# Adding DMAs for the low halves in units 2 to 10 of a decoder layer's feed-forward input, and a fourth pair by seven products in each

## The chip, the cores and the metric

The kernel runs on one core of one Trainium2 chip. The metric is the device time of one execution in microseconds (us); lower is better.

## The reference

One layer of a decoder trunk works on a sequence of 256 rows of 2048 float32 values. It has a token mixer (three kinds of attention with one combined input projection) and then a gated feed-forward part. Only the feed-forward input matters here:

```
gate, up = split(h @ w_ffn_in)        # h: 256 x 2048, w_ffn_in: 2048 x 11264
x = x + gate2 * ((silu(gate) * up) @ w_ffn_out)
```

`h` is the normalised input of this part; gate and up have 5632 columns each.

## The kernel before

**Products in two halves.** TensorE multiplies in a rounded float32 format. To keep the accuracy, each operand is split: a high half (the operand rounded, made by a cast on ScalarE) and a low half (operand minus high half, a subtraction on VectorE). One product of a 128 x 128 piece of `h` and a 128 x 512 piece of a weight is then three matmuls, in `mm3`, lines 172 to 174: high x high, high x low of the weight (L173), low x high.

**Units.** The 5632 columns of gate and of up are done in 11 units of 512 columns. A unit takes 512 columns of gate (`c0`) and the same of up (`c1`), over all 2048 rows of the weight. These rows are 16 pieces of 128, in 8 pairs. Units 0 and 1 run through `block`. Units 2 to 10 (`FAST`) run through `fast_products`, which takes the pairs in the order of a list; each entry of the list is a pair's number and a flag.

- A pair with flag 0 is done *plainly*: two column blocks (gate's, then up's) x two row tiles of `h` x two pieces = 8 products, 24 matmuls. Its two weight blocks of 128 x 1024 values are loaded, cast and subtracted one after the other. The text calls them the pair's first and second block.
- A pair with flag 1 is done *by seven products*, in Strassen's manner: 21 matmuls. For it VectorE first makes sums and differences of the weight blocks (four subtractions of 128 x 512), and then there are three splits of 128 x 1024 and one of 128 x 512. The first of the seven products is collected over all such pairs of the unit in the accumulator `p1`; when the last such pair is done, `p1` is copied on ScalarE (L1430) and four additions on VectorE combine the rest (L1431 to L1434); the halves of the result are added in `merge` (L1390).

Units 2, 3, 5, 6 and 8 (`FOUR`) have four pairs by seven products and four plain (`PAIRS_4`), the units 4, 7, 9 and 10 three and five (`PAIRS`). In both lists a unit's first two pairs are plain.

**Where blocks live.** `load_pair` brings a pair in. `raw_at` (L1334) issues a 512 KB load on SyncE's queue into a buffer for raw weights, of which there are six in turn up to unit 8, five in unit 9 and four in unit 10. `split` takes the next pair of tiles for the two halves, in the text also a room (`whi` and `wlo`, four of each, and further pairs of old tiles: `X1`/`X2` and `A2`/`A3` in all units, `A4`/`A8` up to unit 9, `T4`/`T5` up to unit 6); so there are eight rooms up to unit 6, seven in units 7 to 9 and six in unit 10. It issues the cast on ScalarE (L1354) and the subtraction on VectorE (L1340, through `sub`). A room is free again when TensorE has read both halves for the last time; a raw buffer, when the subtraction has read it.

**Order.** Each engine works through its instructions in one order that the framework's scheduler writes at build time, from priorities; an instruction that waits holds those behind it on its engine. SyncE's loads are such a queue too. GpSimd's queue has nothing in units 2 to 10 but, as unit 2 begins, the last of six DMAs of 512 KB that put tiles away in DRAM (L1239 for `x2`, L1253 for the second gate's sums).

Of the kernel before, what the change touches and what calls it, by code (L numbers as in the profile page):

```python
# [10 lines left out]
F32 = mybir.dt.float32  # L11
# [3 lines left out]
ALU = mybir.AluOpType  # L15
# [7 lines left out]
DFF = 5632  # L23
NB = 512
# [23 lines left out]
OUT_UNITS = (4, 5, 6, 3)  # L48
OUT_A = tuple((p, 0) for p in range(8)) + tuple(x for i in range(6) for x in ((8 + i, 1), (14 + i, 0))) + ((20, 0), (21, 0))
OUT_B = ((0, 0), (1, 0)) + tuple(x for a, b in zip((8, 9, 10, 11, 12, 13, 6, 7), (2, 3, 4, 5, 14, 15, 16, 17)) for x in ((a, 1), (b, 0)))  # L50
PAIRS = ((0, 0), (1, 0), (5, 1), (2, 0), (6, 1), (7, 1), (3, 0), (4, 0))
PAIRS_4 = ((0, 0), (1, 0), (4, 1), (5, 1), (2, 0), (6, 1), (7, 1), (3, 0))
FOUR = (2, 3, 5, 6, 8)
RANK = 16
ROW_N1, ROW_N2, ROW_SBQ, ROW_SBK, ROW_DILQ, ROW_DILK, ROW_GB, ROW_GG = 16, 32, 48, 49, 50, 51, 52, 56

# [23 lines left out]
def trunk(ctx: ExitStack, tc: tile.TileContext, I, out):  # L80
    nc = tc.nc
# [11 lines left out]
    def nm(base):  # L93
        uid[0] += 1
        return f"{base}_{uid[0]}"

    def S(tag, shape, dtype=F32):
        return slot.tile(shape, dtype, tag=tag, name=nm(tag))
# [4 lines left out]
    def scr(shape, dtype=F32):  # L103
        return sp.tile(shape, dtype, tag="scr", name=nm("scr"))

    def acc_bank(shape=None):
        return psa.tile(shape or [P, NB], F32, tag="acc", name=nm("acc"))
# [4 lines left out]
    @contextmanager  # L112
    def prio(offset=AHEAD):

        with tc.high_priority(offset=offset):
            start = tc.cur_priority
            yield
            n = tc.cur_priority - start
        tc.cur_priority += n

    state = {"rate": 0.0}
# [12 lines left out]
    def flush():  # L134
        while bg or after:
            tick(1)


    def load_weights(src, k0, k1, c0, w=NB, spare=(), ahead=True, late=None):

        parts = []
        step = (2 * NB) // w
        with prio() if ahead else nullcontext():
            for ka in range(k0, k1, step):
                n = min(step, k1 - ka)
                raw = wp.tile([P, step, w], F32, tag="raw", name=nm("raw"))
                state["load"] = nc.sync.dma_start(  # L150
                    raw[:, :n, :],
                    src[ka * P : (ka + n) * P, c0 : c0 + w].rearrange("(k p) c -> p k c", p=P),
                )
                i = len(spare) - (k1 - ka)
                if i >= 0:
                    hi = S(spare[i], [P, step, w], F32R)
                    lo = S(spare[i + 1], [P, step, w], F32R)
                else:
                    hi = wp.tile([P, step, w], F32R, tag="whi", name=nm("whi"), bufs=4)
                    lo = wp.tile([P, step, w], F32R, tag="wlo", name=nm("wlo"), bufs=4)  # L160
                if i >= 0 and late is not None:
                    state["casts_after"] = late
                with tc.issue_after(state["casts_after"]) if "casts_after" in state else nullcontext():
                    state["cast"] = nc.scalar.copy(hi[:, :n, :], raw[:, :n, :])  # L164
                state["split"] = nc.vector.tensor_tensor(lo[:, :n, :], raw[:, :n, :], hi[:, :n, :].bitcast(F32), op=ALU.subtract)  # L165
                parts += [(hi[:, i, :], lo[:, i, :]) for i in range(n)]
        if late is not None:
            state.pop("casts_after", None)
        return parts
# [928 lines left out]
    for j in range(2):  # L1098
        hi = S(gtag[0][j], [P, 4, T], F32R)
        lo = S(gtag[1][j], [P, 4, T], F32R)  # L1100
        for t in range(NT):
# [5 lines left out]
            for par in range(2):  # L1107
                gcol = vec[:, ROW_GG + par : ROW_GG + par + 1]
                src = ps[:, par:4:2, :]
# [195 lines left out]
    w_ff = I["w_ffn_in"]  # L1305
# [21 lines left out]
    def load_pair(src, p, c0, c1, fast, tags):  # L1327


        def raw_at(c):  # L1330
            more_raws = state.get("more_raws", ())
            i = state["raws"] = (state.get("raws", -1) + 1) % (4 + len(more_raws))
            raw = S(more_raws[i], [P, 2, NB]) if i < len(more_raws) else wp.tile([P, 2, NB], F32, tag="raw", name=nm("raw"))
            nc.sync.dma_start(raw, src[2 * p * P : (2 * p + 2) * P, c : c + NB].rearrange("(k p) c -> p k c", p=P))  # L1334
            return raw

        def sub(dst, x, y):
            chain = state.get("chain")
            with tc.issue_after(chain.ins) if chain is not None else nullcontext():
                done = nc.vector.tensor_tensor(dst, x, y, op=ALU.subtract)  # L1340
            if "chain" in state:
                state["chain"] = done
            return done

        def split(src):
            n = src.shape[1]
            more_rooms = state.get("more_rooms", ())
            i = state["tiles"] = (state.get("tiles", -1) + 1) % (4 + len(more_rooms))
            if i < len(more_rooms):
                hi, lo = (S(tag, [P, 2, NB], F32R) for tag in more_rooms[i])  # L1350
            else:
                hi = wp.tile([P, 2, NB], F32R, tag="whi", name=nm("whi"), bufs=4)
                lo = wp.tile([P, 2, NB], F32R, tag="wlo", name=nm("wlo"), bufs=4)
            nc.scalar.copy(hi[:, :n, :], src)  # L1354
            state["split"] = sub(lo[:, :n, :], src, hi[:, :n, :].bitcast(F32))
            return [(hi[:, i, :], lo[:, i, :]) for i in range(n)]

        with prio():
            if not fast:
                return [split(raw_at(c0)), split(raw_at(c1))]  # L1360
            r0, r1 = raw_at(c0), raw_at(c1)
            b11, b21 = split(r0)
            ta, tb = (S(tag, [P, 2, NB]) for tag in tags)
            sub(ta[:, 0], r1[:, 0], r0[:, 0])
            sub(ta[:, 1], r1[:, 1], r1[:, 0])
            (b22,) = split(r1[:, 1:2])
            sub(tb[:, 0], r1[:, 1], ta[:, 0])
            sub(tb[:, 1], r0[:, 1], tb[:, 0])
            t1, t3 = split(ta)
            t2, t4 = split(tb)  # L1370
            return b11, b21, b22, t1, t3, t2, t4
# [71 lines left out]
    def rooms_until(i, rooms):  # L1443
        return tuple(tags for tags, end in rooms if i < end)

    def fast_unit(i):
        own, other = (acc_bank, misc_bank) if i % 2 else (misc_bank, acc_bank)
        return fast_products(w_ff, i * NB, DFF + i * NB, PAIRS_4 if i in FOUR else PAIRS, h2_at, h2s, own, other, ("OD", "KD"))

    ring["tags"] = ("A12", "KD", "KC", "T0", "A7", "A11")  # L1450
    act = []
    for i in range(NFF):
        if i == FAST[0]:
            flush()
        state["more_rooms"], state["more_raws"] = rooms_until(i, MORE_ROOMS), rooms_until(i, MORE_RAWS)
        if i in FAST:
            pg, pu = fast_unit(i)
        else:
            state["rate"] = RATES_FFN[2 * i]
            pg = [acc_bank() for _ in range(NT)]  # L1460
        if i in FAST:
            pass
        elif i == 0:
            w = load_weights(w_ff, 0, KC, 0, spare=("A9", "A10", "A0", "A1", "T1", "T2", "T4", "T5"), late=state["late_casts"])
            state["loads_after"] = state["load"].ins
            for t in range(NT):
                block(pg, h2_at, None, 0, KC, 0, w=w, tiles=(t,), steps=None if t else {N2_AT[1]: lambda: norm2_turn(1, xs)}, pace=0.5)
        else:
            block(pg, h2_at, w_ff, 0, KC, i * NB)
        if i == 0:  # L1470
            h2s = sums_of_h2()
        sgs = []
        with prio():
            for t in range(NT):
                sg = scr([P, NB])
                nc.scalar.activation(sg, pg[t], AF.Silu)
                sgs.append(sg)
        if i not in FAST:
            state["rate"] = RATES_FFN[2 * i + 1]
            state.pop("loads_after", None)  # L1480
            pu = [acc_bank() for _ in range(NT)]
            block(pu, h2_at, w_ff, 0, KC, DFF + i * NB)
        if ftags[2 * i] == ftags[2 * i + 1]:
            hl = S(ftags[2 * i], [P, 2, 4, T], F32R)
            hi, lo = hl[:, 0], hl[:, 1]
        else:
            hi, lo = (S(tag, [P, 4, T], F32R) for tag in ftags[2 * i : 2 * i + 2])
        with prio():
            for t in range(NT):
                nc.vector.tensor_mul(sgs[t], sgs[t], pu[t])  # L1490

        def turn(sgs=sgs, hi=hi, lo=lo, bank=acc_bank if i % 2 else misc_bank):
            for t in range(NT):
                transpose_split(sgs[t], hi, lo, t, bank)

        later.append(turn)
        act.append((hi, lo))
# [87 lines left out]
    n, pss = 3, o[1]  # L1585
# [42 lines left out]
```

## Time and profile before

| | before |
|---|---|
| median of 3 runs | 1578.32 us (1578.15 to 1579.47) |
| the profiled execution | 1578.33 us |
| its span, first to last instruction | 1576.4 us |
| granted TensorE clock | 1.00 |
| TensorE busy | 1565.7 us (99%) |
| VectorE busy | 1354.7 us (86%) |
| ScalarE busy | 862.3 us (55%) |
| GpSimd busy | 12.4 us (1%) |
| DMA, mean over the span | 255 GB/s |

Engines in the rows: PE is TensorE's matmuls, PEld its weight loads (they overlap), DVE is VectorE, ACT ScalarE, POOL GpSimd, SP SyncE. Times count from the span's start. A row of a timeline has the start, the duration, the engine, the line, the operation and the tiles as written<-read, with buffer numbers left out: `whi<-ada` is a cast from the raw buffer `ada`. A row of a group ends with its number (x51) and its durations in ns (least, median, most). A matmul row lasts 0.39 us though the next starts 0.23 us later, since they are pipelined.

### The profile page before, as it was taken

The page shows a single profiled execution, that of the slowest core. Times are in us where ns is not written, and L with a number is a line of the kernel's source. Part 1 is how long each engine was busy: PE and PEld are TensorE (multiplying, and loading weights), DVE is VectorE, ACT ScalarE, POOL GpSimd, SP SyncE. Part 2 cuts the span into 40 slices and gives each one's busy share as a digit, 9 for nine tenths or more (in the row PEclk, how much of TensorE's full clock was granted, in tenths as well). Part 3 has the DMA queues.
Part 4 walks back from the last instruction along what each step waited for, and adds up shares of the span by engine and source line. Part 5 has one row for each costly group of instructions (what it writes and reads, how often), then busy time and mean ns, then how long its engine had stood idle before and what let it go on. Part 6 is the DMA issues. An engine that isn't in the chain of part 4 may idle for free.

```text
span 1576.4 us, 20198 instructions
## 1 busy us (share of the span) xinstructions
PE 1565.7 (99%) x7204; PEld 1297.2 (82%) x7204; DVE 1354.7 (86%) x1640; ACT 862.3 (55%) x1196; POOL 12.4 (1%) x24
## 2 busy tenths in 40 slices
PE   8999999999999999999999999999999999999998
PEld 7878888888888888888888888888888888888887
DVE  6889996888888687877777888999999999999996
ACT  5654448875754444444444645556565555455553
POOL 1000000000000000000000000000000000000000
PEclk9999999999999999999999999999999999999999
DMA  9999987677788899879877886565566566876664
GB/s 334 359 327 322 336 305 247 213 225 229 236 278 269 293 322 325 305 269 312 274 270 234 302 305 215 188 213 187 194 211 209 174 200 235 287 229 200 224 211 136
DMA packets 196315, 402.24 MB, mean 255 GB/s; under 512 B 13102, under 2 KB 28116, under 8 KB 196216
## 3 DMA queue, kind: packets, MB, share of 16 engines
q1 hardware_dynamic: 194952, 397.75, 74.8%
q0 software_dynamic: 1088, 3.16, 0.5%
q8 instruction: 56, 0.92, 0.2%
q14 instruction: 43, 0.35, 0.1%
q10 hardware_dynamic: 176, 0.07, 0.0%
HBM read 395.68 MB, written 5.24 MB: 254 GB/s over the span
## 4 chain that ended last, share of the span: by engine, by line
PE 95%; ACT 2%; DVE 1%; issue 1%; DMA 0%; POOL 0%; ACTq 0%; POOLq 0%; DVEq 0%
PE acc L174 23%; PE acc L173 23%; PE acc L172 23%; PE misc L172 7%; PE misc L174 7%; PE misc L173 7%; PE acc L454 1%; PE misc L823 1%; PE misc L1137 1%; PE misc L447 0%; DVE wlo L165 0%; DMA H<-c 0%; PE misc L349 0%; ACT whi L164 0%; PE acc L1137 0%
## 5 line engine op out<-in xcount | busy, mean ns | idle before, releaser
L164 ACT CAST whi<-raw 128x1024 fp32r<-128x1024 f32 x325 | 329.9, 1018 | 357.6 <-PE acc L174 258.2
L165 DVE TENSOR_TENSOR wlo<-raw,whi 128x1024 fp32r<-128x1024 f32 x325 | 380.8, 1179 | 142.1 <-ACT whi L164 140.7
L172 PE MATMUL acc<-whi,H 128*128 128x512 f32 (+1 forms) x1117 | 437.1, 392 | 0.9 <-ACT H L466 0.8
L173 PE MATMUL acc<-wlo,H 128*128 128x512 f32 (+1 forms) x1117 | 435.5, 390 | 0.8 <-DVE wlo L165 0.7
L174 PE MATMUL acc<-whi,H 128*128 128x512 f32 (+1 forms) x1117 | 435.5, 390 | 0.5 <-DVE H L473 0.4
L174 PEld LDWEIGHTS acc<-whi,H 128*128 128x128 f32 x1117 | 209.5, 188 | 45.2 <-DVE H L473 1.6
L172 PEld LDWEIGHTS acc<-whi,H 128*128 128x128 f32 x1117 | 209.7, 188 | 44.0 <-ACT H L466 1.3
L173 PEld LDWEIGHTS acc<-wlo,H 128*128 128x128 f32 x1117 | 209.9, 188 | 43.8 <-DVE wlo L165 1.7
L1354 ACT CAST whi<-raw 128x1024 fp32r<-128x1024 f32 (+1 forms) x104 | 99.3, 969 | 49.0 <-PE acc L174 23.5
L1340 DVE TENSOR_TENSOR wlo<-raw,whi 128x1024 fp32r<-128x1024 f32 (+1 forms) x104 | 114.0, 1119 | 10.7 <-ACT whi L1354 9.6
L174 PE MATMUL acc<-whi,A 128*128 128x512 f32 x222 | 86.5, 390 | 0.0
L172 PE MATMUL acc<-whi,A 128*128 128x512 f32 x212 | 83.0, 391 | 0.0
L173 PE MATMUL acc<-wlo,A 128*128 128x512 f32 x212 | 82.5, 389 | 0.0
L299 DVE SCALAR_TENSOR_TENSOR ada<-AR,csil,ada 128x1024 f32<-128x1024 f32 x39 | 49.7, 1281 | 4.9 <-DMA AR<-w_ada 4.9
L174 PE MATMUL misc<-whi,H 128*128 128x512 f32 (+1 forms) x131 | 50.6, 386 | 0.0
L173 PE MATMUL misc<-wlo,H 128*128 128x512 f32 (+1 forms) x131 | 50.5, 386 | 0.0
L172 PE MATMUL misc<-whi,H 128*128 128x512 f32 (+1 forms) x131 | 50.5, 386 | 0.0
L174 PEld LDWEIGHTS acc<-whi,A 128*128 128x128 f32 x222 | 41.7, 188 | 8.7
L173 PEld LDWEIGHTS acc<-wlo,A 128*128 128x128 f32 x212 | 39.8, 188 | 8.1
L172 PEld LDWEIGHTS acc<-whi,A 128*128 128x128 f32 x212 | 39.8, 188 | 8.1
L1340 DVE TENSOR_TENSOR A<-raw,A 128x1024 fp32r<-128x1024 f32 (+2 forms) x41 | 40.7, 1002 | 3.1 <-ACT A L1354 2.7
L1354 ACT CAST whi<-OD 128x1024 fp32r<-128x1024 f32 (+1 forms) x25 | 25.5, 1020 | 30.2 <-DVE OD L1340 16.7
(639 smaller groups left out, 2815.2 us busy)
## 6 DMA issues: line engine op xcount, KB each, us to landing
raw<-w_in SPq DMA_DIRECT2D x205, 512.0 KB, 5.0
raw<-w_ffn_in SPq DMA_DIRECT2D x135, 512.0 KB, 4.6
raw<-w_ffn_out SPq DMA_DIRECT2D x73, 512.0 KB, 5.1
AR<-w_ada SPq DMA_DIRECT2D x58, 512.0 KB, 4.9
raw<-w_out SPq DMA_DIRECT2D x32, 512.0 KB, 5.3
OS<-w_ada SPq DMA_DIRECT2D x24, 512.0 KB, 6.2
KC<-w_ada SPq DMA_DIRECT2D x23, 512.0 KB, 4.7
AR<-w_ffn_in SPq DMA_DIRECT2D x22, 512.0 KB, 5.1
```

The source lines that it names most:

```text
L164: state["cast"] = nc.scalar.copy(hi[:, :n, :], raw[:, :n, :])
L165: state["split"] = nc.vector.tensor_tensor(lo[:, :n, :], raw[:, :n, :], hi[:, :n, :].bitcast(F32), op=ALU.subtract)
L172: nc.tensor.matmul(ps, lh, rh, start=start, stop=False, skip_group_check=seeded)
L173: nc.tensor.matmul(ps, lh, rl, start=False, stop=False, skip_group_check=seeded)
L174: state["mm"] = nc.tensor.matmul(ps, ll, rh, start=False, stop=stop, skip_group_check=seeded)
L299: nc.vector.scalar_tensor_tensor(acc, raw, c, acc, op0=ALU.mult, op1=ALU.add)
L454: state["warm"] = nc.tensor.matmul(ps, ones_r, wide, start=True, stop=True)
L823: nc.tensor.matmul(ps[:n, t * N_GLA + h, :].rearrange("p (s l) -> p s l", l=L), at(f, h, t)[:, :n], odd(at(f, h, t)), start=True, stop=True,)
L1137: nc.tensor.transpose(ps[:, i, :], src[:, i * P : (i + 1) * P], ident)
L1340: done = nc.vector.tensor_tensor(dst, x, y, op=ALU.subtract)
L1354: nc.scalar.copy(hi[:, :n, :], src)
```

## The change

Three things, in one piece. All nine units use the list with four pairs by seven products. In `load_pair`, a plain pair's second block gets its low half in another way: ScalarE casts the high half as before, then writes the negated high half into the low half's tile, and a DMA on GpSimd's queue adds the raw block onto that tile in place. And this is switched on for units 2 to 10 alone, not for the feed-forward's output, which uses the same functions. Lines behind the lists stand two lower after the change, those behind `split` two higher.

```
-PAIRS = ((0, 0), (1, 0), (5, 1), (2, 0), (6, 1), (7, 1), (3, 0), (4, 0))
-PAIRS_4 = ((0, 0), (1, 0), (4, 1), (5, 1), (2, 0), (6, 1), (7, 1), (3, 0))
-FOUR = (2, 3, 5, 6, 8)
+PAIRS = ((0, 0), (1, 0), (4, 1), (5, 1), (2, 0), (6, 1), (7, 1), (3, 0))
...
-        def split(src):
+        def split(src, by_dma=False):
...
             nc.scalar.copy(hi[:, :n, :], src)
-            state["split"] = sub(lo[:, :n, :], src, hi[:, :n, :].bitcast(F32))
+            if by_dma:
+                nc.scalar.mul(lo[:, :n, :], hi[:, :n, :].bitcast(F32), -1.0)
+                nc.gpsimd.dma_start(lo[:, :n, :].bitcast(F32), src, accum_op=ALU.add)
+            else:
+                state["split"] = sub(lo[:, :n, :], src, hi[:, :n, :].bitcast(F32))
...
-                return [split(raw_at(c0)), split(raw_at(c1))]
+                return [split(raw_at(c0)), split(raw_at(c1), state.get("adds", False))]
...
-        return fast_products(w_ff, i * NB, DFF + i * NB, PAIRS_4 if i in FOUR else PAIRS, h2_at, h2s, own, other, ("OD", "KD"))
+        return fast_products(w_ff, i * NB, DFF + i * NB, PAIRS, h2_at, h2s, own, other, ("OD", "KD"))
...
         if i in FAST:
+            state["adds"] = True
             pg, pu = fast_unit(i)
+            state["adds"] = False
```

## The prediction

> **What bounds the kernel now.** I read the page first, then busy time by stage, and then the timelines of TensorE and ScalarE inside the units that change.
>
> ```profile
> span 1576.4 us, 20198 instructions
> PE 1565.7 (99%) x7204; PEld 1297.2 (82%) x7204; DVE 1354.7 (86%) x1640; ACT 862.3 (55%) x1196; POOL 12.4 (1%) x24
> q0 software_dynamic: 1088, 3.16, 0.5%
> PE 95%; ACT 2%; DVE 1%; issue 1%; DMA 0%; POOL 0%; ACTq 0%; POOLq 0%; DVEq 0%
> ```
>
> TensorE is busy 99% of the span, and 95% of the chain that ended last is TensorE. The profiled execution took 1578.33 us, 1.9 more than its span; the median of the runs is 1578.32, so I add changes straight to that.
>
> ```profile
> core 0: us, PE busy (x) PEld busy (x) DVE busy (x) ACT busy (x) POOL busy (x), PEclk, DMA share, GB/s
> 960.00:1340.00 380.00, 379.95 (x1713) 314.97 (x1712) 365.46 (x446) 220.46 (x252) 0.00 (x0) 1.00 0.60 201
> 1380.00:1420.00 40.00, 40.00 (x178) 33.10 (x177) 36.65 (x39) 22.07 (x23) 0.00 (x0) 1.00 0.71 231
> ```
>
> The first row is units 2 to 10. TensorE idles 0.05 us there; VectorE is at 96%, ScalarE at 58%, GpSimd empty, the DMA engines at 60%, the granted clock full. So VectorE is nearly full and yet nobody waits for it in the end. The second row is a stretch of 512-column products alone: 40 us hold 177 weight loads, 0.226 us a product. TensorE runs at its own pace, and only two things can move the end: the number of products, and a wait put into TensorE's queue.
>
> **What the change takes off.** A pair done plainly has 8 products of two halves, each three matmuls: 24. By seven products it is 21. Units 4, 7, 9 and 10 get a fourth such pair: 4 x 3 = 12 matmuls fewer, 12 x 0.226 = 2.7 us. With no idle TensorE to win back this is all there is to gain, 0.17%. About 0.2% (3.2 us) is what a measurement of this kernel can tell from no change, so the gain alone stays under it.
>
> ```profile
> L1340 DVE TENSOR_TENSOR wlo<-raw,whi x51: 682/1219/1234, 959.6 to 1336.1; 128x1024 fp32r<-128x1024 f32 x40, 128x512 fp32r<-128x512 f32 x11
> L1340 DVE TENSOR_TENSOR KD<-raw,KD x22: 683/687/697, 960.9 to 1320.1; 128x512 f32<-128x512 f32 x22
> L1354 ACT CAST whi<-raw x51: 613/1051/1059, 974.4 to 1337.2; 128x1024 fp32r<-128x1024 f32 x41, 128x512 fp32r<-128x512 f32 x10
> ```
>
> VectorE loses 36 subtractions of 1.22 us (one for each of the 36 plain pairs left) = 43.9 us. Four pairs turned from plain to seven products cost it one more full subtraction and five half ones each, 1.22 + 5 x 0.69 = 4.7, in all 18.6. Net 25 us less of 365; worth nothing by itself, since TensorE did not wait for it. ScalarE gains 36 negations, bounded by its full casts at 1.05 us, 38 us, and 4 x (1.05 + 0.61) = 7 us of casts: 220 becomes 265 of 380 us, free as busy time but not in its order (below).
>
> **What the change adds to a wait.** For the second block of a plain pair the low half is now ready after: cast, negation, a DMA on GpSimd's queue that adds, its landing. The matmul of L173 waits for the landing, and behind it all of TensorE's in-order queue. GpSimd's queue itself is empty (0.00 above), so nothing stands behind its waits. SyncE's queue does: a raw buffer is free only when the DMA has landed, and the load waiting for it holds all later loads.
>
> No adding DMA is in this trace. The nearest rows are the 512 KB DMAs that GpSimd issues from the same memory to DRAM:
>
> ```profile
> L1239 POOL DMA_DIRECT2D x<-A x4: 533/534/566, 807.0 to 873.3; - x4
> DMA to landing us min/median/max: 6.1/6.9/8.1
> ```
>
> ```profile
> L1253 POOL DMA_DIRECT2D gate<-T x1: 533/533/533, 957.6 to 957.6; - x1
> DMA to landing us min/median/max: 5.7/5.7/5.7
> ...
> DMA to landing us min/median/max: 3.2/4.5/5.7
> ```
>
> The 5.7 is that DMA's own; the last line is for both DMAs of L1253, of which the other went out at 943.5.
>
> Lower end: 3.2 us, the faster of the two gate DMAs. Upper end: 8.1, the slowest put-away, plus a second read. That read of the destination is bounded by the queue row of the page (1088 packets, 3.16 MB, 0.5% of 16 engines): 3.16 MB took 0.5% of 1576.4 us on 16 engines, 7.9 us, so 512 KB take 1.3 us; 8.1 + 1.3 = 9.4. I take the last one, gate<-T, which runs as unit 2 begins (5.7), plus 1.3: 7.0 us from issue to landing. The Trainium skill, "Collectives: The Full Stack", section on the bandwidth ceiling, says that an add in a DMA costs no time for the arithmetic but needs two source reads on one ring, and so runs at half the rate of a copy. An estimate by it doubles the transfer's part, which is the same 1.3 us; no row here shows it.
>
> Now the slack there is. Second blocks, in order of time, first what ScalarE does (unit 3's third plain pair, unit 3's fourth, unit 8's fourth, unit 10's fourth):
>
> ```profile
> 1017.26 1.05 ACT L1354 CAST whi<-ada 128x1024 fp32r<-128x1024 f32 x1
> ...
> 1033.22 1.05 ACT L1354 CAST whi<-ada 128x1024 fp32r<-128x1024 f32 x1
> 1034.17 1.05 ACT L1354 CAST X<-raw 128x1024 fp32r<-128x1024 f32 x1
> ...
> 1036.07 0.58 ACT L1430 COPY T<-misc 128x512 f32<-128x512 f32 x1
> ...
> 1242.78 1.99 ACT L1354 CAST A<-raw 128x1024 fp32r<-128x1024 f32 x2
> ...
> 1324.08 1.06 ACT L1354 CAST whi<-raw 128x1024 fp32r<-128x1024 f32 x1 [0.30 <-PE misc L174]
> 1325.04 0.57 ACT L1430 COPY T<-acc 128x512 f32<-128x512 f32 x1
> 1325.51 1.05 ACT L1354 CAST X<-raw 128x1024 fp32r<-128x1024 f32 x1
> ```
>
> and then TensorE's first use of the low half of each:
>
> ```profile
> 1026.98 0.39 PE L173 MATMUL acc<-wlo,H 128*128 128x512 f32 x1
> 1034.68 0.39 PE L174 MATMUL misc<-A,H 128*128 128x512 f32 x1
> 1041.94 0.39 PE L173 MATMUL acc<-wlo,H 128*128 128x512 f32 x1
> 1252.20 0.39 PE L173 MATMUL misc<-A,H 128*128 128x512 f32 x1
> 1331.54 0.39 PE L173 MATMUL misc<-wlo,H 128*128 128x512 f32 x1
> ```
>
> ScalarE starts a cast 0.95 us after the last (1033.22 to 1034.17). In each case I put the negation where the changed program's order on ScalarE has it:
> - Unit 3, third plain pair: right behind the cast. 1017.26 + 0.95 + 1.05 = 1019.26; used at 1026.98: slack 7.7 us.
> - Unit 3, fourth plain pair: behind the next cast and behind L1430's copy of the first product, which waits for the matmul that closes it (1034.68 + 0.39 = 1035.07). Cast at 1034.17, copy from 1035.12, and 0.48 later (as 1325.04 to 1325.51) the negation, done 1036.65; used at 1041.94: 5.3 us. Units 3 to 6 have this order.
> - Unit 8, fourth: the second of two casts starts at 1243.73 (0.95 in), negation done 1245.73, used at 1252.20: 6.5 us. Units 7 to 9 have one room pair less than units 2 to 6; I use it for their third pairs too.
> - Unit 10, fourth: copy between, negation 1325.51 to 1326.56, used at 1331.54: 5.0; its third pair, no copy, 5.5.
> - First and second pairs come behind the merge and the transposes, with several us more; unit 2's and the other third pairs have 7.7.
>
> At 7.0 us TensorE waits 1.7 in each of units 3 to 6 (6.8), 0.5 in six places of units 7 to 9 (3.0), 2.0 + 1.5 in unit 10: 13.3 us. Each wait is new, since rooms are freed by TensorE itself and a stall does not help the next block. Net 13.3 - 2.7 = 10.6: **1588.9 us**.
>
> The loads stay covered at this price:
>
> ```profile
> 1020.40 0.37 SPq L1334 DMA_DIRECT2D ada<-w_ffn_in  x1
> ...
> DMA to landing us min/median/max: 3.3/4.5/6.8
> ```
>
> This load went out when unit 3's third second block had been subtracted, and its cast is the one at 1033.22. Issued at 1019.26 + 7.0 = 1026.3 it lands at 1030.8, 2.4 us early. At 9.4 that cover is gone.
>
> **The rivals.**
> - *Hidden.* The adding DMA lands in 5 us or less: DMA engines are at 60% in these units, a load (from DRAM, by SyncE) lands in 4.5, and the 3.2 us row is of the same kind. Every slack is then enough, and the 12 matmuls show: 1578.3 - 2.7 = 1575.6, not slower. Between, the waits sum to 4(T - 5.3) + (T - 5.0) + (T - 5.5) up to T = 6.5; at T = 6.3 they are 6.1, net +3.4, so up to about 6.3 the result stays within 0.2%. Against it: five of six rows are 5.7 or more, and none reads twice.
> - *Long landing.* 9.4 us. Then 1.7 in six places (unit 2 and the third pairs of units 3 to 6), 4.1 x 4, 2.9 x 6 and 4.4 + 3.9: 52.3, net +49.6, 1627.9, and the loads begin to be late as well. For it: VectorE was busy 8.91 of 9 us around the 8.1 us put-away and 3.51 of 4 around the 3.2 us one, in the rows below, and is at 96% here. Against it: the DMA share was 0.94 there, which alone may be the cause, and VectorE gets 25 us lighter. The Trainium skill, "SBUF — State Buffer", section "SBUF: two separate sides", says that descriptors of a GpSimd DMA cannot be written while VectorE holds the shared port in a two-port mode; by it these two-input subtractions should not hold them up, and no row here parts the two causes.
>
> ```profile
> 873.00:882.00 9.00, 9.00 (x49) 7.44 (x48) 8.91 (x18) 5.21 (x14) 0.53 (x1) 1.00 0.94 337
> 943.00:947.00 4.00, 4.00 (x20) 3.30 (x19) 3.51 (x4) 1.34 (x2) 0.53 (x1) 1.00 0.81 263
> ```
>
> - *Not what it says.* The order of the changed program has the 36 DMAs and 12 matmuls fewer, so I give this nothing.
>
> **How the numbers follow.** Forecast (6.3 to 8.7 us): 0.5. Within 0.2% (up to 6.3): 0.27. Long (over 8.7): 0.18. Faster by over 0.2%: 0.05, for the hidden case with the spread of 1.3 us that the three runs have; no row gives it otherwise. So slower 0.68. Range: low 1575.5, the hidden case. High at T = 8.7: 1.0 x 6 + 3.4 x 4 + 2.2 x 6 + 3.7 + 3.2 = 39.7, net 37, 1615. Above it I leave out about 0.18. The forecast's own range is 1582 to 1615.
>
> **What would show it.** In the profile of the changed kernel: 12 matmuls fewer; GpSimd with 36 more DMAs and their landing time, the one number on which all hangs; idle TensorE in front of L171, which is L173 moved up by the change's two dropped lines, released by a DMA that writes wlo, A, X or T, twice a unit, longest in units 3 to 6's fourth plain pair and in unit 10; VectorE near 340 us in the units' stretch. I am wrong if the landing is under 6.3 us, if the waits stand before other operands (late loads, the cast chain of the seven products), or if they don't repeat from unit to unit.

## The result, and the profile after

The changed kernel took 1616.14 us (median of 4 runs, 1615.32 to 1618.88), the kernel before beside it 1578.41: 1.0241 times as long, 95% interval 1.0223 to 1.0259, or 37.7 us more. The forecast was 10.6 us more. The profiled execution has a span of 1613.5 us, 37.1 more than before.

The page of the changed kernel (span, engines, the queue of GpSimd's DMAs, the chain by engine):

```profile
span 1613.5 us, 20347 instructions
PE 1577.7 (98%) x7192; PEld 1297.7 (80%) x7192; DVE 1332.8 (83%) x1628; ACT 900.0 (56%) x1240; POOL 43.9 (3%) x60
q0 software_dynamic: 6272, 22.04, 6.9%
PE 15%; DMA 2%; DVE 0%; issue 0%; POOLq 0%; DVEq 0%; SPq 0%
```

The 12 matmuls are gone (7204 to 7192), VectorE is 22 us lighter, and DMA now stands in the chain. (The shares of this chain add up to 17% of the span only, those of the chain before to 99%.) Busy time by stage, columns as in the prediction's row of 960 to 1340 us, first units 2 to 10, then what follows:

```profile
960.00:1378.00 418.00, 392.27 (x1707) 316.37 (x1707) 346.17 (x439) 256.70 (x295) 29.65 (x34) 0.98 0.79 226
1378.00:1580.00 202.00, 202.00 (x897) 167.27 (x896) 185.47 (x209) 110.16 (x118) 0.00 (x0) 1.00 0.71 233
```

All of the loss is in units 2 to 10: TensorE, which idled 0.05 us of 380, now idles 26 of 418. The waits of TensorE there (tile written, line, what released it: us in total, times, longest):

```profile
PE misc L171 <- DMA wlo<-raw: 6.5, 3, 4.1
PE acc L170 <- DVE A L200: 5.3, 3, 2.1
PE misc L170 <- DVE T L200: 2.8, 1, 2.8
PE misc L170 <- DVE A L200: 2.0, 1, 2.0
PE misc L171 <- DMA wlo<-ada: 1.8, 1, 1.8
PE misc L1135 <- DVE scr L1494: 1.1, 1, 1.1
PE acc L170 <- DVE T L200: 1.1, 1, 1.1
PE acc L170 <- DVE OS L200: 1.0, 2, 0.7
PE misc L170 <- DVE ada L200: 1.0, 2, 0.7
```

There are two kinds. L171 waits for an adding DMA, as forecast. L170 (high x high) waits for L200, VectorE's low-half subtraction of the *previous* unit's transposed gate: the seven products' shared accumulators take the PSUM banks of those transposes, and are free only when L200 has read them. The waits of before had none of this kind. Idle time starts at the modelled end of a matmul; counted from start to start against 0.227 us, over all records from 955 to 1390 us, the loss is 13.8 us at L171 for DMAs, 15.0 at L170, 5.4 in matmuls that run at half rate after long waits, 2.2 at the transposes (L1135) and 3.1 elsewhere: 39.5, against 1.2 before. These figures the expectations use too.

**A wait of the forecast kind**, unit 10's fourth plain pair, on TensorE's timeline; from the third row on they start 0.43 us apart, where before the wait it was 0.23:

```profile
1367.95 0.39 PE L170 MATMUL misc<-whi,H 128*128 128x512 f32 x1
1372.43 0.80 PE L171 MATMUL misc<-wlo,H 128*128 128x512 f32 x1 [4.09 <-DMA wlo<-raw]
1373.02 0.63 PE L172 MATMUL misc<-whi,H 128*128 128x512 f32 x1
1373.44 0.63 PE L170 MATMUL misc<-whi,H 128*128 128x512 f32 x1
```

**A wait of the other kind**, unit 3, back along its chain. TensorE:

```profile
1020.80 0.39 PE L171 MATMUL misc<-A,AR 128*128 128x512 f32 x1
1023.22 0.47 PE L170 MATMUL misc<-whi,AR 128*128 128x512 f32 x1 [2.03 <-DVE A L200]
```

VectorE comes to L200 late. It had idled for a load and for a cast, and is busy without a break from 1014.17 on:

```profile
1000.77 0.69 DVE L1338 TENSOR_TENSOR OD<-raw,raw 128x512 f32<-128x512 f32 x1 [1.56 <-DMA raw<-w_ffn_in]
...
1014.17 1.23 DVE L1338 TENSOR_TENSOR wlo<-KD,whi 128x1024 fp32r<-128x1024 f32 x1 [0.91 <-ACT whi L1352]
...
1022.39 0.68 DVE L200 TENSOR_TENSOR A<-misc,A 128x512 fp32r<-128x512 f32 x1
1022.99 0.68 DVE L1338 TENSOR_TENSOR KD<-raw,OD 128x512 f32<-128x512 f32 x1
```

The cast of 1014.17 stood on ScalarE behind this one, which had waited for a load:

```profile
1011.59 0.62 ACT L1352 CAST A<-raw 128x512 fp32r<-128x512 f32 x1 [1.93 <-DMA raw<-w_ffn_in]
```

In the kernel before the same subtraction (there L202) stood at:

```profile
1013.95 0.69 DVE L202 TENSOR_TENSOR A<-misc,A 128x512 fp32r<-128x512 f32 x1
```

SyncE, whose loads come out late (in the kernel before `ada` was loaded at 997.75):

```profile
1003.66 0.37 SPq L1332 DMA_DIRECT2D raw<-w_ffn_in  x1
1010.63 0.37 SPq L1332 DMA_DIRECT2D ada<-w_ffn_in  x1
```

And why: the two adding DMAs of unit 3's first pairs went out at 996.71 and 1000.51 and landed at 1003.6 and 1010.6, and each held its raw buffer until then, with all loads behind it. The load of 1003.66 is the one that the cast of 1011.59 waited for:

```profile
996.71 0.86 POOL L1355 DMA_DIRECT2D A<-raw  x1 [2.44 <-ACT A L1354]
1000.51 0.86 POOL L1355 DMA_DIRECT2D T<-ada  x1 [2.93 <-ACT T L1354]
...
DMA to landing us min/median/max: 4.9/6.4/10.6
```

(The last line is that of all 36 adding DMAs.) What SyncE's queue waited for, over units 2 to 10, the three largest:

```profile
SPq L1332 <- DVE KD L1338: 101.9, 43, 7.6
SPq L1332 <- DMA wlo<-raw: 68.2, 15, 7.3
SPq L1332 <- DVE wlo L1338: 66.7, 26, 7.2
```

With `wlo<-ada`, `T`, `X` and `A` it is 158 us of waiting for adding DMAs; before, it waited almost only for VectorE. That sum alone proves little: with the small DMA of `e3_tiny` below it is still 110 us. What tells more is that ScalarE's casts waited 45 us for loads of `w_ffn_in` from 955 to 1390 us, and 12 us before.

### The profile page after: what moved, and what is told of

The parts are those of the page before. It is cut to its first block, busy times and chain, and to the rows that moved or that the text cites. A ratio compares the mean times of both kernels' runs of the same rounds, so it can differ in the third digit from the quotient of the medians.

```text
span 1613.5 us, 20347 instructions
## 1 busy us (share of the span) xinstructions
PE 1577.7 (98%) x7192; PEld 1297.7 (80%) x7192; DVE 1332.8 (83%) x1628; ACT 900.0 (56%) x1240; POOL 43.9 (3%) x60
## 5 line engine op out<-in xcount | busy, mean ns | idle before, releaser
L170 PE MATMUL acc<-whi,H 128*128 128x512 f32 x1096 | 429.1, 392 | 0.9 <-ACT H L464 0.8
L171 PE MATMUL acc<-wlo,H 128*128 128x512 f32 x1096 | 428.0, 390 | 1.7 <-DMA wlo<-raw 0.9
L172 PE MATMUL acc<-whi,H 128*128 128x512 f32 x1096 | 427.6, 391 | 0.5 <-DVE H L471 0.4
L171 PEld LDWEIGHTS acc<-wlo,H 128*128 128x128 f32 x1096 | 206.1, 188 | 45.8 <-DMA wlo<-raw 2.1
L172 PEld LDWEIGHTS acc<-whi,H 128*128 128x128 f32 x1096 | 205.7, 188 | 44.3 <-DVE H L471 1.6
L170 PEld LDWEIGHTS acc<-whi,H 128*128 128x128 f32 x1096 | 205.9, 188 | 43.1 <-ACT H L464 1.3
L1352 ACT CAST whi<-raw 128x1024 fp32r<-128x1024 f32 (+1 forms) x110 | 103.8, 956 | 66.3 <-PE acc L172 19.0
L1338 DVE TENSOR_TENSOR wlo<-raw,whi 128x1024 fp32r<-128x1024 f32 (+1 forms) x95 | 102.2, 1086 | 14.2 <-ACT whi L1352 13.1
L171 PE MATMUL acc<-wlo,A 128*128 128x512 f32 x210 | 81.8, 390 | 0.0
L170 PE MATMUL acc<-whi,A 128*128 128x512 f32 x210 | 81.7, 391 | 0.0
L171 PE MATMUL misc<-wlo,H 128*128 128x512 f32 (+1 forms) x162 | 64.3, 397 | 8.5 <-DMA wlo<-raw 6.5
L170 PE MATMUL misc<-whi,H 128*128 128x512 f32 (+1 forms) x162 | 63.7, 393 | 0.0
L172 PE MATMUL misc<-whi,H 128*128 128x512 f32 (+1 forms) x162 | 63.5, 392 | 0.0
L171 PEld LDWEIGHTS acc<-wlo,A 128*128 128x128 f32 x210 | 39.4, 188 | 8.5 <-DVE wlo L163 0.5
L170 PEld LDWEIGHTS acc<-whi,A 128*128 128x128 f32 x210 | 39.4, 188 | 8.1
L171 PEld LDWEIGHTS misc<-wlo,H 128*128 128x128 f32 x162 | 31.1, 192 | 17.3 <-DMA wlo<-raw 8.8
```

The source lines that it names most:

```text
L170: nc.tensor.matmul(ps, lh, rh, start=start, stop=False, skip_group_check=seeded)
L171: nc.tensor.matmul(ps, lh, rl, start=False, stop=False, skip_group_check=seeded)
L172: state["mm"] = nc.tensor.matmul(ps, ll, rh, start=False, stop=stop, skip_group_check=seeded)
```

## The experiments

Three theories were held against each other. Theory 1 is the prediction's: the adding DMA is late at L171, and nothing else. Theory 2: L200 is late because the scheduler now puts it behind more of VectorE's subtractions. Theory 3: adding DMAs hold raw buffers and fill the DMA engines, loads are late, VectorE with them, and L200 with VectorE.

**Each part alone, the size of the DMA, the order.**

`e1_pairs_only`: the pair lists of the change, no adding DMA.

```
-            state["adds"] = True
+            state["adds"] = False
```

> The pair lists of the change alone: four pairs by seven products in all nine units, every low half by VectorE, no adding DMA. Theory 1 (the whole loss is the adding DMAs' lateness at L171): the loss goes and the 12 matmuls show, 1578.4 - 2.7 = 1575.7 us. Theory 2 (the loss at L170 comes of where the previous unit's low-half subtractions, L200, stand in VectorE's order, which the shorter fast list moves by itself): no wait at L171 for a DMA, but waits at L170 for L200 as in the changed kernel, 15 us and some half-rate matmuls behind them; and VectorE, 365.5 us busy of 380 before, would be given 18.6 more, 384, so units 2 to 10 cannot take less than about 384: 1582 at the least, up to about 1597. Theory 3 (the loss at L170 comes of raw loads that wait for adding DMAs): no such waits, 1575.7, or 1582 if VectorE itself becomes the bound.

Measured: 1591.63 us (1.0074, 1.0059 to 1.0089).

```profile
960.00:1380.00 420.00, 411.54 (x1825) 336.33 (x1824) 405.10 (x496) 236.25 (x273) 0.00 (x0) 0.99 0.63 200
PE acc L170 <- ACT whi L1352: 6.4, 4, 4.0
```

VectorE is at 96% of 420 us, and TensorE waits for the cast chain of the seven products (the second row). The 12 matmuls do not show: with VectorE full, four such pairs in every unit cost 12 us, not -2.7. The relief that the prediction held to be worth nothing is what this part lives on.

`e2_adds_only`: adding DMAs, the pair lists of before.

> The adding DMAs of the change alone, with the pair lists of before (four pairs by seven in units 2, 3, 5, 6, 8, three in the others): 40 adding DMAs, no matmul fewer. Theory 1: the waits at L171 as in the changed kernel, about 14 us, and nothing at L170: 1592 us. Theories 2 and 3: the waits at L170 for L200 come back as well, since L200 stands here as late in VectorE's order as in the changed kernel (behind 18 subtractions of the unit) and the loads wait for the DMAs as there: 14 + 15 + 5 of half-rate matmuls + 3, 1612 to 1618 us.

Measured: 1621.57 us (1.0257, 1.0233 to 1.0280). VectorE has some 49 us less to do than before (40 subtractions of 1.22), and the kernel is 42 us slower.

```profile
960.00:1380.00 420.00, 392.72 (x1690) 318.49 (x1689) 325.33 (x408) 252.44 (x287) 33.08 (x38) 0.96 0.81 228
PE acc L1137 <- DVE scr L1496: 8.5, 4, 3.6
```

From start to start: 11.1 us at the DMAs, 7.7 at L202, 14.4 at transposes that wait for VectorE (the last row), 10.1 at half rate. VectorE is idle for 95 of 420 us and yet late. The total is near what theories 2 and 3 gave (1612 to 1618), but the waits are in other places. So the adding DMAs alone make the loss.

`e3_tiny`: the adding DMA adds only 64 columns.

```
-                nc.gpsimd.dma_start(lo[:, :n, :].bitcast(F32), src, accum_op=ALU.add)
+                nc.gpsimd.dma_start(lo[:, :1, :64].bitcast(F32), src[:, :1, :64], accum_op=ALU.add)
```

> The changed kernel, in which each adding DMA adds only 64 columns of one half of its block (32 KB in place of 512): most of the addition is left out, the order, the negations and the number of DMAs are kept. Tells a long landing from the order. Theory 1: the landing falls from 6.4 to some 2 to 3 us, every slack (5.0 us and more) is then enough, and the loss goes: about 1576 us. Theory 2: the waits at L171 go (13.8 us), those at L170 for L200 stay (15.0, and about 4 of half-rate matmuls behind them), 1576 + 19 + up to 3 of other small waits: 1595 to 1598 us. Theory 3: the loads no longer wait long for a DMA, VectorE is on time, both kinds go: 1576 to 1580 us, with VectorE's order as in the changed kernel.

Measured: 1583.78 us (1.0027, 1.0017 to 1.0037). The waits and the landing:

```profile
PE misc L171 <- DMA wlo<-raw: 4.1, 1, 4.1
PE acc L170 <- DVE A L200: 1.2, 1, 1.2
DMA to landing us min/median/max: 2.1/3.5/6.9
```

The waits at L170 fell from 15.0 us to 1.9, though VectorE's and ScalarE's order is the changed kernel's but for a few neighbours at the end. So the order alone is not the cause, and theory 2 as it stands falls. But the order has its share. Unit 3's L200 is here at

```profile
1020.07 0.69 DVE L200 TENSOR_TENSOR A<-misc,A 128x512 fp32r<-128x512 f32 x1
```

and TensorE does not wait for it. That is 6 us later than the 1013.95 of the kernel before, with VectorE busy without a break since 998.50: the new order used up L200's slack, and in the changed kernel the late data put it 2.3 us further, to 1022.39. Of the 38 us, 32 hang on the DMA's size; of what stays over 1575.7, 4.1 is one wait, in unit 10.

`e5_turn_first`: the transposes and L200 taken earlier.

```
-                with tc.issue_after(state["mm"].ins), prio():
+                with tc.issue_after(state["mm"].ins), prio(3 * AHEAD):
                     later.pop()()
```

> The changed kernel with the transposes of the previous unit's gate and their L200 subtractions given a higher priority, so that on VectorE L200 stands behind 6 subtractions of the unit and not behind 18. Theory 1: nothing or little, about 1614 to 1616 us. Theory 2: the waits at L170 (15.0 us) and the half-rate matmuls behind them (about 4) go, those at L171 (13.8) stay: 1595 to 1598 us. Theory 3: VectorE is late because loads are late; L200 taken earlier then only makes other subtractions late, and the wait moves to the low halves of other blocks: 1608 to 1616 us.

Measured: 1626.15 us (1.0294, 1.0277 to 1.0311), slower than any theory had it.

```profile
PE misc L171 <- DMA wlo<-raw: 10.5, 4, 4.2
PE acc L171 <- DMA wlo<-raw: 8.5, 3, 3.7
DMA to landing us min/median/max: 5.1/7.2/10.5
```

From start to start L170 has 0.2 us left, L171 34.8, and 13.0 go in half-rate matmuls. The waits at L170 can be ordered away, but the time is not won: more is then lost at L171, before adding DMAs. That it is the same lateness in another place is a reading that fits, and not shown.

**Which property of the DMA.**

`e4_neg_first`: each negation right behind its cast.

```
-                nc.scalar.mul(lo[:, :n, :], hi[:, :n, :].bitcast(F32), -1.0)
+                with prio(4 * AHEAD):
+                    nc.scalar.mul(lo[:, :n, :], hi[:, :n, :].bitcast(F32), -1.0)
```

> The changed kernel with each negation given a higher priority, so that ScalarE does it right behind its cast and not behind the next cast and a copy (units 3 to 6 and 10, fourth plain pair). Theory 1 (the landing is late at L171, nothing else): the waits of those five places shrink by the 2.4 us that the negation comes earlier, so of 13.8 us at L171 about 6 stay and the loss at L170 with its half-rate matmuls goes on: 1616 - 8 = 1608 us. Theory 3 (adding DMAs hold raw buffers until they land, so loads are late, VectorE is late, and L200 with it): the buffers of those five blocks come free 2.4 us earlier as well, a little less is lost at L170: 1600 to 1608 us. If the landing grows because the DMAs now go out in a busier moment: no change, 1614 to 1618.

Measured: 1619.47 us (1.0262, 1.0246 to 1.0277): no gain. In unit 3 the negation ended 2.9 us behind its cast's start and not 4.6, and its DMA landed 7.5 us after that and not 5.4: the landing took the gain back. In units 4 to 6 the negation gained only 0.4 to 1.2 us and the landing lost 1.1 to 1.8; in unit 10 nothing stood between cast and negation that could be gained. The loss at L171 is 16.2 us, at L170 14.3.

`e11_dram`: the same bytes added, read from DRAM.

```
-                nc.gpsimd.dma_start(lo[:, :n, :].bitcast(F32), src, accum_op=ALU.add)
+                nc.gpsimd.dma_start(lo[:, :n, :], state["dram"].bitcast(F32R), accum_op=ALU.add)
...
```

> The changed kernel, with the adding DMA reading the weights a second time from DRAM and not from the raw buffer: as many bytes, but a raw buffer is free as soon as ScalarE has cast it. Tells what holds the loads. Theory 3 with the buffers held as the cause: loads are early again, the 15.0 us at L170 and most of the half-rate matmuls go, the 13.8 at L171 stay: 1578.4 - 2.7 + 14 to 18 = 1590 to 1594 us. Theory 3 with the traffic as the cause (the DMA engines at 79% in place of 60%, so loads land late): the loss at L170 stays, 1605 to 1616 us. Theory 1 alone: the landing decides; a load from DRAM has a median of 4.7 us, and if an add from DRAM is as quick the waits at L171 shrink too, about 1580.

Measured: 1622.98 us (1.0278, 1.0263 to 1.0293).

```profile
PE misc L171 <- DMA wlo<-w_ffn_in: 14.2, 6, 5.9
DMA to landing us min/median/max: 5.6/9.3/12.1
```

Loads no longer wait for adding DMAs, and L170 has 0.6 us. But the landing grew from 6.4 to 9.3 us, and L171 has 35.3, with 9.6 at half rate. The gain of one went into the other; the scheduler's order differs too, so this one alone does not settle the holding.

`e12_dram_lo`: the same, and the negated half made from the raw block ahead of the cast.

```
+                with prio(4 * AHEAD):
+                    nc.scalar.mul(lo[:, :n, :], src, -1.0)
             nc.scalar.copy(hi[:, :n, :], src)
...
```

> As the kernel that adds from DRAM, and the negated high half is made from the raw block itself, ahead of the cast and with a higher priority, so that the adding DMA goes out about 1.05 us earlier at every block and 3.5 earlier where a cast and a copy stood between. If held buffers and the landing are the two causes, both are relieved: slack at L171 becomes 6.3 us and more against a median of 6.4, so most waits go and a few long landings stay: 1576 to 1584 us. If the traffic is the cause: 1600 us or more. If the negations now wait for rooms at the head of ScalarE's queue and hold the casts behind them, waits appear at L170 for casts: over 1590.

Measured: 1614.67 us (1.0226, 1.0211 to 1.0241): 8 us better than the one above, over 30 worse than hoped, since the landing was again 9.0 us in the median where the sum had been made with 6.4. L171 has 27.3, L170 2.5.

`e13_serial`: the small DMA twice, in series.

```
-                nc.gpsimd.dma_start(lo[:, :n, :].bitcast(F32), src, accum_op=ALU.add)
+                nc.gpsimd.dma_start(lo[:, :1, :64].bitcast(F32), src[:, :1, :64], accum_op=ALU.add)
+                nc.gpsimd.dma_start(lo[:, :1, :64].bitcast(F32), src[:, :1, :64], accum_op=ALU.add)
```

> The kernel with 32 KB in place of 512 KB in each adding DMA, with that small DMA done twice, one after the other on the same columns (most of the addition is left out): traffic as in that kernel, but the low half is ready, and the raw buffer free, only after two landings of 3.5 us, about 7 us. Held buffers and late landing as the causes: the loss of the changed kernel comes back without its traffic, 1605 to 1620 us. Traffic as the cause: as the kernel with one small DMA, 1582 to 1588 us.

Measured: 1606.02 us (1.0179, 1.0162 to 1.0196). A DMA share of 0.65 and loads that land in 3.6 us, and still 22 us more than with one small DMA: lateness (and holding) by itself, with the traffic taken away. L171 has 24.0 us, L170 0.9.

`e22_traffic`: one small DMA, and 512 KB of other traffic.

```
...
+                nc.gpsimd.dma_start(spots[state["spot"]], hi[:, :n, :].bitcast(F32))
```

> The kernel with 32 KB in each adding DMA (most of the addition is left out; 1583.8 us), with a second DMA behind each that writes 512 KB, the cast high half, to DRAM, where nobody reads it: the traffic of the changed kernel is back, the low half is ready and the raw buffer free as early as with the small DMA alone; the compute engines' order is the changed kernel's. Traffic alone as the cause of the waits at L170 (loads land later, so VectorE is late): 1595 to 1600 us, with 10 us or more at L170. Traffic and holding only together: 1584 to 1588 us, under 4 us at L170.

Measured: 1599.74 us (1.0135, 1.0120 to 1.0150).

```profile
PE misc L171 <- ACT whi L1354: 5.3, 1, 5.3
PE misc L170 <- DVE A L200: 2.4, 1, 2.4
PE misc L170 <- DVE T L200: 2.4, 1, 2.4
```

L170 is back with 7.4 us, half of the changed kernel's. The small DMA itself now lands in 5.1 us, so it isn't traffic with all else held still: the traffic makes every landing longer, of adds and of loads (5.1 us against 4.5), and so the raw buffers were held longer too: SyncE waited 139 us for adding DMAs, against 110 with the small DMA alone.

`e17_hold`: one small DMA for the low half, two more to hold the raw buffer.

```
...
+                for _ in range(2):
+                    nc.gpsimd.dma_start(junk, src[:, 0, :64])
```

> With 32 KB in each adding DMA (most of the addition is left out), and behind it two more DMAs of 32 KB, one after the other, that read the raw block into a tile nobody uses: the low half is ready after one small landing of some 3.5 us, the raw buffer free only after two more, about 7 to 8 us; the order of every compute engine's queue is that of the changed kernel. With the kernel of one small DMA (1583.8 us) and that of two in series (1606.0 us) it parts the low half's lateness from the buffers' holding. Holding alone as the cause of the 22 us between those two: 1600 to 1608 us, waits at L170 and on late loads. Lateness at L171 alone: 1584 to 1588 us.

Measured: 1602.75 us (1.0149, 1.0133 to 1.0165), but it did not do what it was for.

```profile
POOL junk L1358 <- DMA raw<-w_ffn_in: 118.7, 15, 12.3
```

The two holding DMAs went ahead of the adding one, as soon as the raw block had landed, and it queued behind them on GpSimd. Inconclusive.

`e18_late`: one small DMA from the raw block, one from a constant tile.

```
...
+                nc.gpsimd.dma_start(lo[:, 0, :64].bitcast(F32), ident[:, :64], accum_op=ALU.add)
```

> The counterpart: one small adding DMA from the raw block (which is free after that, some 3.5 us), then a second small one that adds from a constant tile onto the same columns (the output is not the reference's), so the low half is ready only after two landings, about 7 us; the compute engines' order is that of the changed kernel. Lateness at L171 alone as the cause: 1600 to 1606 us, with 14 to 24 us of waits at L171. Holding alone: 1584 to 1588 us. If the two only hurt together, both this and the other stay under 1592.

Measured: 1642.39 us (1.0402, 1.0359 to 1.0444). The low half was later than meant: 9.5 us behind the end of the negation in the mean. It is the strongest sign for lateness (L171 40.0, 14.6 at half rate, a DMA share of 0.62), but as the partner of the one above it fails with it.

The mean time from the end of the negation to the last landing on the low half, over the 36 blocks, from the rows of ScalarE and GpSimd, beside the time. The two rise together only roughly:

| | negation's end to landing | DMA share | us |
|---|---|---|---|
| one small DMA | 4.1 | 0.68 | 1583.8 |
| small, with traffic | 5.5 | 0.75 | 1599.7 |
| small, behind two that hold (`e17_hold`) | 6.2 | 0.66 | 1602.8 |
| the changed kernel | 7.1 | 0.79 | 1616.1 |
| negation first (`e4_neg_first`) | 7.4 | 0.77 | 1619.5 |
| L200 earlier (`e5_turn_first`) | 7.5 | 0.78 | 1626.2 |
| two small in series | 7.6 | 0.65 | 1606.0 |
| add from DRAM (raw buffer not held) | 9.3 | 0.78 | 1623.0 |
| two small, one from a constant | 9.5 | 0.62 | 1642.4 |

How late the loads were can be read on ScalarE, whose casts wait for them. From 955 to 1390 us it waited for loads of `w_ffn_in` 13 us with one small DMA, 22 with two in series, 30 with the small DMA and traffic, and 45 in the changed kernel; TensorE's waits at L170 were 1.9, 0.9, 7.4 and 15.0 us. So longer holding with little traffic, and traffic with less holding, each make loads later, and both together most. That the waits at L170 come of holding alone is not shown: with two in series they were 0.9 us, though there TensorE was itself 24 us late by L171, which gives VectorE time.

**Fewer adds, fewer buffers.**

`e7_two` and `e20_one`: adding DMAs for the first two plain pairs, and for the first alone (`p == 0` there).

```
-                return [split(raw_at(c0)), split(raw_at(c1), state.get("adds", False))]
+                return [split(raw_at(c0)), split(raw_at(c1), state.get("adds", False) and p < 2)]
```

> The changed kernel with the adding DMA only for plain pairs 0 and 1, the third and fourth pair's low halves by VectorE as before: 18 adding DMAs in place of 36. VectorE's work is 365.5 + 18.6 - 18 x 1.22 = 362 us, as before the change. Theory 1: pairs 0 and 1 have several us more slack than a median of 6.4 takes, no wait at L171, the 12 matmuls show: 1575.7 us. Theory 3 (holding): half as many raw buffers are held, half the loss, about 1597 us. Both together, with the DMA engines less full: 1578 to 1590.

> The same for pair 0 alone: 9 adding DMAs, VectorE at 365.5 + 18.6 - 9 x 1.22 = 373 us. Theory 1: 1575.7 us, no wait at L171. Theory 3: a quarter of the loss, 1585 us. If a nearly full VectorE costs by itself (the kernel of the pair lists alone, 384 us of work, took 1591.6): between that and the kernel with two pairs, 1580 to 1588.

Measured: 1585.06 us (1.0038, 1.0024 to 1.0052) and 1593.42 (1.0092, 1.0077 to 1.0107). Two pairs are the best of the versions with whole low halves; one pair is as slow as none (1591.63), VectorE being full again (396.7 of 420 us). With one pair 7.3 us also go at L171 for the adding DMAs of that first pair, in six places, though the prediction gave first pairs several us more of slack. None beats the kernel before, and the most to be had is the 2.7 us of the matmuls, under what can be told from no change.

`e24_not10`: `state["adds"] = i < 10`.

> The changed kernel with adding DMAs in units 2 to 9 only; unit 10, which has four raw buffers where the others have six or five, makes its four low halves by VectorE. In the changed kernel unit 10 lost 4.5 + 1.5 us at L171, 4.1 at L170 and some 2 in half-rate matmuls. If these come of held buffers being short there: all of it goes, 1616 - 12 = 1604 us. If what is late in unit 10 was late already when it began (VectorE behind since the units before): only the 6 us at L171 go, 1610 us.

Measured: 1609.07 us (1.0180, 1.0160 to 1.0199). 7 us come back, about what unit 10 lost at L171 (4.3 and 1.3) with the half-rate matmuls behind it (6 of them, 1.2); L170 keeps about 14, of which 13 are for L200. The waits at L170 are not a matter of the last unit's four buffers.

`e25_before_raws`: the kernel before, `MORE_RAWS = ()`.

> The kernel before with four raw buffers in all units and not six, five and four: no adding DMA at all. Prices late loads by themselves. If holding a raw buffer longer is what makes VectorE and L200 late, taking two of six buffers away does it too: 5 to 25 us slower, 1584 to 1604, with waits at L170's counterpart L172 for L202. If the loads have slack enough with four: 1578 to 1580, and holding four of sixteen blocks some 6 us longer can't be the cause by itself.

Measured: 1589.65 us (1.0069, 1.0053 to 1.0084).

```profile
PE acc L172 <- DVE T L202: 1.8, 2, 1.2
PE misc L172 <- DVE T L202: 1.1, 1, 1.1
PE acc L172 <- DVE A L202: 0.9, 1, 0.9
```

With no adding DMA at all, raw buffers that run short bring the same kind of wait, 4.8 us of them from start to start, and 11 us in all. ScalarE waited 55 us for loads of `w_ffn_in`, against 12. That is theory 3's last link by itself.

## Why the prediction was wrong

- *The matmuls.* 12 fewer, 0.226 us each: as forecast, and paid back many times.
- *The landing.* Forecast 7.0 us; measured 6.4 from issue to landing in the median, 7.1 in the mean from the end of the negation, from which the slack was counted. Right.
- *The waits at L171.* Forecast 13.3 us, measured 13.8. Right in kind, and in the fourth pairs of units 4 to 6 (1.4, 1.1 and 2.0 for 1.7 each). That the sum fits so well is in part luck: unit 10's fourth pair lost 4.3, forecast 2.0, and unit 3's, forecast 1.7, lost 0.2, as its DMA landed in 5.1 us.
- *"The loads stay covered at this price."* This is the step that failed. It followed one load to its own cast, 2.4 us early, and made that the whole cover. Here the load behind unit 3's third pair went out at 1028.55 and not at 1026.3, and its cast ran at 1036.6 and not 1033.2. But the load that decided unit 3's wait was the one behind the unit's *first* pair, a block dismissed because "several us more" of slack stood before its own use. Its buffer was held to 1003.6, and the load that then went out there was for a pair by seven products, whose casts and subtractions stand ahead of L200. (The load behind the second pair was held to 1010.6, but VectorE did not idle after 1014.17, so nothing shows that L200 waited for it. The other units' waits were not followed back in this way.) Slack of a block at TensorE says nothing about its raw buffer.
- *The missing terms.* 15.0 us at L170, 5.4 at half rate, 5.3 at the transposes and elsewhere: 25.7, against 27.2 by which the forecast was low. The prediction had no term for L200: neither for its later place in VectorE's order, which took 6 us of its slack in unit 3, nor for late data. The small DMA (15.0 down to 1.9) and the kernel before with four buffers (4.8 with no add) show that late data are needed for the waits. How much of it is the holding and how much the fuller DMA engines stays open. In unit 3 the load that decided landed 5.9 us later than with the small DMA: it went out 2.4 us later (1003.66 for 1001.22) and took 7.8 us for 4.4. Over the whole, from one small DMA the traffic gives 16 us and the longer landing on top of it another 16, while two small ones in series give 22 with little traffic. The run made to part the two, `e17_hold`, did not.
- *VectorE.* 340 us forecast for the units' stretch, 346 measured. "Worth nothing by itself" was wrong as a judgement of the change: without it the pair lists alone cost 12 us. And a lighter VectorE was no safer: it is lighter and later.
- *The rivals.* "Long landing" named late loads, at 9.4 us, and did not price them; they came at 6.4. The range ended at 1615 because it counted L171 alone.

The prediction had named the sign: it would be wrong if the waits stood before other operands, late loads among them. That is what happened.

## What to carry to other kernels

A step moved from an engine to a DMA is to be costed twice: when its result is needed, and when its *source* is free again; the second sets the loads, and through an in-order load queue every later block, also those with plenty of slack of their own. An engine's busy time does not tell whether it is on time: VectorE lost 22 us of work here and became the one that is waited for. And where two late things feed one queue, taking away one wait (an order, an earlier issue, a held buffer) shows it again at the other, so compare totals and not single waits.

## What the runs showed of the hardware

- An adding DMA of 512 KB costs the DMA engines about as much as two copies of that size to DRAM: q0's time went from 7.9 us (0.5% of 1576.4 us, six DMAs, 1.3 us each on all 16 engines) to 111.3 (6.9% of 1613.5), 103.4 more for 36, 2.9 us each. Its issue holds GpSimd for 0.87 us where a copy took 0.53. A sixteenth of the bytes only about halves the landing: 32 KB took 2.1 us at best and 3.5 in the median, 512 KB 4.9 and 6.4. The Trainium skill, "DMA: Bandwidth & Descriptors", section "Anatomy of one DMA — SWDGE (gpsimd) path", gives a GpSimd DMA a fixed 2.0 us and 436 GB/s beyond, 2.1 us for 32 KB; the fastest one here agrees, the median does not, with loads on the same engines.
- After a wait TensorE's matmuls can run at half rate: 0.427 us from start to start, as in the rows from 1373.02 on, for some 3 us. In the changed kernel 27 of them cost 5.4 us. They followed waits of 4.25, 2.9 and 2.24 us, and of two waits of 2.19 us they followed one (at 1020.8) and not the other (1066.8). The granted clock (the third figure from the end) shows the same: 0.57 behind the wait of 4.25 us, 0.58 behind that at 1020.8, 1.00 behind that at 1066.8.

```profile
1372.00:1376.00 4.00, 3.57 (x9) 2.88 (x10) 1.03 (x2) 0.67 (x2) 0.00 (x0) 0.57 0.58 154
1025.00:1028.00 3.00, 3.00 (x9) 2.33 (x9) 3.00 (x4) 2.67 (x4) 0.00 (x0) 0.58 0.72 143
1069.00:1072.00 3.00, 2.81 (x12) 2.36 (x13) 3.00 (x6) 1.93 (x3) 0.32 (x1) 1.00 1.04 268
```

  The Trainium skill, "TensorE: Matmul & The Clock Gate", section "What's actually happening", puts the gate at half clock after an idle window of about 3.4 us; here less than that sufficed.
